# Where the weight parts, the normed rows and the activations lie in SBUF, in a four-layer decoder trunk

## The chip, the cores and the metric

The kernel runs on one core of one Trainium2 chip, as one launch. The metric is the device time of that launch in microseconds (us). The kernel before was timed three times: 1962.36, 1965.19 and 1966.22 us, median 1965.19 us. Shorter is better. All durations below come from one further execution that the hardware profiler recorded; its span is 1960.8 us.

## What is computed

Four decoder layers on 256 tokens of 1024 features, all in float32. Each layer is half a SwiGLU feed-forward, a token mixer, and another half feed-forward; a norm closes the trunk. The mixers are stick-breaking attention (layers 0 and 3), MoBA attention (layer 1) and latent attention (layer 2). Cut to what matters here:

```python
D_MODEL, SEQ, DEPTH, D_FF = 1024, 256, 4, 2816
def swiglu(x, w_gate_up, w_down):
    g, u = jnp.split(x @ w_gate_up, 2, axis=-1)
    return (jax.nn.silu(g) * u) @ w_down

for i in range(DEPTH):
    h = h + 0.5 * swiglu(rms_norm(h, norm_ffn1[i]), ffn1_w_gate_up[i], ffn1_w_down[i])
    h = h + mixer_i(rms_norm(h, norm_mix[i]))          # kind i mod 3
    h = h + 0.5 * swiglu(rms_norm(h, norm_ffn2[i]), ffn2_w_gate_up[i], ffn2_w_down[i])
return rms_norm(h, final_norm)
```

The weights are about 340 MB of float32, read once. The eight feed-forwards hold most of them and most of the products.

## The kernel before, in words

**Split products.** TensorE takes operands of the type float32r. Each float32 value is split into a high part (its rounding to float32r) and a low part (the rest), and a product of two float32 values becomes three products of parts: high by high, high by low, low by high. The hidden state `h` lies transposed, features on the 128 partitions and the 256 tokens along the columns.

**Weights.** A `Chunk` is up to 1 MB of one weight matrix. Its DMA lands in one of four buffers `raw` (8192 bytes in each partition). ScalarE then writes the high parts to a buffer `whi` (L314), VectorE subtracts and writes the low parts to a buffer `wlo` (L321). A `whi` and a `wlo` (4096 bytes in each partition) are taken and given back as a pair; there are six such pairs, in the list `parts`.

**Feed-forward.** `ffn` computes 22 column blocks of gate and up from the normed rows `x2`, then 8 row blocks of the output from the activations `a2`. Both tiles hold, for each row block of 128 features, 256 columns of high parts and then 256 columns of low parts. The helper `wide` issues two products for a 128x128 piece of weights: the piece's high part stays in the array while all 512 columns of the row block stream through (L434), then its low part while the 256 high columns stream (L435). This text calls the two a *pair*. The kernel has 4224 pairs. Each product is preceded by a load of its 128x128 weights (LDWEIGHTS, the rows of PEld), 512 bytes in each partition.

**Mixers.** `mm3` does the three products one by one, 256 columns each (L428, L429, L430; 512 such triples), for queries, keys and the output projection. `x_proj` does it the other way round: 128 columns of the normed rows are loaded as weights, and up to 512 columns of `whi` or `wlo` stream (L475, L476, L477; 232 triples).

**Order.** `Program` is a list scheduler: it puts all instructions of all engines in order by estimated costs before anything is built. The addresses of tiles play no part in it. DMAs are issued by SyncE.

**Addresses.** Tiles are laid out one after the other in the order in which `cp.tile` is called, each rounded up to 32 bytes. Nearly all tiles have sizes that are multiples of 512 bytes. The tile `gh` (gains and `h`) has 8628 bytes, and `x2` and `a2` follow it. In the built program a partition's addresses are therefore:

| tile | before: address, and modulo 1024 | after: address, and modulo 1024 |
|---|---|---|
| whi0 | 49280, 128 | 49280, 128 |
| wlo0 | 53376, 128 | 73920, 192 |
| whi1, wlo1 | 57472, 128 and 61568, 128 | 53376, 128 and 78016, 192 |
| x2 | 151104, 576 | 98496, 192 |
| a2 | 167488, 576 | 114880, 192 |

All six `whi` agree modulo 1024 with the first, all six `wlo` too, and row blocks of `x2` and `a2` are 2048 bytes apart. A 128x128 piece of weights starts at a multiple of 512 bytes within its buffer.

The program is allocated here:

## Time and profile before

| what | value |
|---|---|
| median of three timed runs | 1965.19 us (1962.36 to 1966.22) |
| span of the profiled execution | 1960.8 us |
| TensorE products busy | 1946.6 us, 99% |
| TensorE weight loads busy | 1696.5 us, 87% |
| VectorE busy | 1452.3 us, 74% |
| ScalarE busy | 1144.1 us, 58% |
| mean rate of the DMAs | 175 GB/s, q1 50.6% of 16 engines |
| granted TensorE clock | 0.998 of full speed |

How to read it: PE are products, PEld their weight loads, DVE is VectorE, ACT ScalarE. A product is drawn from when its columns enter until its last result is out, so successive products overlap in the table of times, and the duration of one is longer than the distance from its start to the next start. That distance, the *step*, is what a product costs when TensorE never idles. The chain of waits follows the work that ended last back to its beginning.

### The profile page before, as it was taken

The page shows a single profiled execution, that of the slowest core. Times are in us where ns is not written, and L with a number is a line of the kernel's source. Part 1 is how long each engine was busy: PE and PEld are TensorE (multiplying, and loading weights), DVE is VectorE, ACT ScalarE, POOL GpSimd, SP SyncE. Part 2 cuts the span into 40 slices and gives each one's busy share as a digit, 9 for nine tenths or more (in the row PEclk, how much of TensorE's full clock was granted, in tenths as well). Part 3 has the DMA queues.
Part 4 walks back from the last instruction along what each step waited for, and adds up shares of the span by engine and source line. Part 5 has one row for each costly group of instructions (what it writes and reads, how often), then busy time and mean ns, then how long its engine had stood idle before and what let it go on. Part 6 is the DMA issues. An engine that isn't in the chain of part 4 may idle for free.

```text
span 1960.8 us, 30578 instructions
## 1 busy us (share of the span) xinstructions
PE 1946.6 (99%) x11681; PEld 1696.5 (87%) x11681; DVE 1452.3 (74%) x2661; ACT 1144.1 (58%) x2119; POOL 0.4 (0%) x5
## 2 busy tenths in 40 slices
PE   9999999999999999999999999999999999999997
PEld 7888989888888878888888888988888888898886
DVE  8777767777777777877677768877677766668864
ACT  7555556555555555655555557755555555665553
POOL 0000000000000000000000000000000000000000
PEclk9999999999999999999999999999999999999999
DMA  8546435546654653554655454355465456435542
GB/s 301 184 146 220 163 129 175 191 147 204 208 181 147 221 181 109 178 188 147 214 199 191 141 178 155 126 197 178 151 213 197 165 168 220 148 125 198 177 151 81
DMA packets 55875, 342.79 MB, mean 175 GB/s; under 512 B 6192, under 2 KB 7088, under 8 KB 26928
## 3 DMA queue, kind: packets, MB, share of 16 engines
q1 hardware_dynamic: 55728, 340.84, 50.6%
q8 instruction: 92, 1.51, 0.3%
q14 instruction: 55, 0.45, 0.1%
HBM read 339.76 MB, written 1.05 MB: 174 GB/s over the span
## 4 chain that ended last, share of the span: by engine, by line
PE 98%; ACT 1%; DVE 0%; DMA 0%; SPq 0%; issue 0%; DVEq 0%; ACTq 0%
PE ps L434 50%; PE ps L435 26%; PE ps L428 3%; PE ps L429 3%; PE ps L430 3%; PE ps L475 3%; PE ps L476 2%; PE ps L477 2%; PE ps L574 1%; PE ps L624 1%; PE ps L733 1%; PE ps L698 1%; PE ps L771 1%; PE ps L596 1%; PE ps L562 0%; PE ps L576 0%
## 5 line engine op out<-in xcount | busy, mean ns | idle before, releaser
L314 ACT ACTIVATE whi<-raw 128x1024 fp32r<-128x1024 f32 (+2 forms) x738 | 703.0, 954 | 729.7 <-PE ps L434 527.3
L321 DVE TENSOR_TENSOR wlo<-raw,whi 128x1024 fp32r<-128x1024 f32 (+2 forms) x738 | 804.2, 1091 | 396.7 <-ACT whi L314 388.6
L434 PE MATMUL ps<-x,whi 128*128 128x512 f32 x2816 | 998.3, 398 | 1.0 <-DVE acc L345 0.8
L435 PE MATMUL ps<-x,wlo 128*128 128x256 f32 x2816 | 791.8, 281 | 0.2 <-DVE wlo L321 0.2
L434 PEld LDWEIGHTS ps<-x,whi 128*128 128x128 f32 x2816 | 529.7, 188 | 132.2 <-ACT whi L314 2.5
L435 PEld LDWEIGHTS ps<-x,wlo 128*128 128x128 f32 x2816 | 528.8, 188 | 1.3 <-DVE wlo L321 1.2
L434 PE MATMUL ps<-a,whi 128*128 128x512 f32 x1408 | 498.8, 398 | 0.0
L435 PE MATMUL ps<-a,wlo 128*128 128x256 f32 x1408 | 395.7, 281 | 0.0
L434 PEld LDWEIGHTS ps<-a,whi 128*128 128x128 f32 x1408 | 264.8, 188 | 65.1
L435 PEld LDWEIGHTS ps<-a,wlo 128*128 128x128 f32 x1408 | 264.4, 188 | 0.0
L443 DVE TENSOR_TENSOR mid<-ps,mid 128x256 f32<-128x256 f32 x416 | 173.5, 417 | 9.6 <-ACT mid L442 9.6
L442 ACT ACTIVATE mid<-ps 128x256 f32<-128x256 f32 x416 | 151.3, 367 | 11.9 <-PE ps L435 11.9
L515 DVE TENSOR_TENSOR mid<-mid 128x256 f32<-128x256 f32 x176 | 74.6, 424 | 14.2 <-DVE mid L443 0.5
L510 DVE TENSOR_TENSOR mid<-mid,rb 128x256 f32<-128x256 f32 x176 | 74.7, 424 | 6.4 <-ACT rb L411 0.9
L475 PE MATMUL ps<-whi,x 128*128 128x512 f32 (+2 forms) x192 | 74.4, 388 | 0.0
L517 DVE TENSOR_TENSOR a<-mid,a 128x256 fp32r<-128x256 f32 x176 | 73.4, 418 | 1.0 <-ACT a L516 1.0
L428 PE MATMUL ps<-a,whi 128*128 128x256 f32 x256 | 73.9, 289 | 0.0
L428 PE MATMUL ps<-x,whi 128*128 128x256 f32 x256 | 73.0, 285 | 0.0
L476 PE MATMUL ps<-wlo,x 128*128 128x512 f32 (+2 forms) x192 | 72.9, 380 | 0.0
L511 ACT ACTIVATE mid<-mid 128x256 f32<-128x256 f32 x176 | 71.8, 408 | 1.8 <-DVE mid L510 1.7
L477 PE MATMUL ps<-whi,x 128*128 128x512 f32 (+2 forms) x192 | 72.7, 379 | 0.0
L429 PE MATMUL ps<-a,whi 128*128 128x256 f32 x256 | 71.5, 279 | 0.0
(128 smaller groups left out, 1636.7 us busy)
## 6 DMA issues: line engine op xcount, KB each, us to landing
raw<-in_ffn_gu SPq DMA_DIRECT2D x173, 1024.0 KB, 4.8
raw<-in_ffn_dn SPq DMA_DIRECT2D x128, 704.0 KB, 4.1
raw<-in_sb_qk SPq DMA_DIRECT2D x16, 1024.0 KB, 4.9
raw<-in_moba_qkv SPq DMA_DIRECT2D x12, 1024.0 KB, 4.8
raw<-in_sb_v SPq DMA_DIRECT2D x8, 1024.0 KB, 4.7
raw<-in_sb_o SPq DMA_DIRECT2D x8, 1024.0 KB, 4.7
raw<-in_moba_o SPq DMA_DIRECT2D x4, 1024.0 KB, 4.8
raw<-in_mla_o SPq DMA_DIRECT2D x4, 1024.0 KB, 5.0
```

The costliest lines, as they stand in the source:

```text
L314: return lambda: nc.scalar.activation(b.ap[0][:, (k - i) * w:(e - i) * w], raw.ap[:, k * w:e * w], AF.Copy)
L321: nc.vector.tensor_sub(b.ap[1][:, s], raw.ap[:, k * w:e * w], b.ap[0][:, s].bitcast(F32))
L428: nc.tensor.matmul(o, wh, mh, start=first, stop=False, skip_group_check=True)
L429: nc.tensor.matmul(o, wh, ml, start=False, stop=False, skip_group_check=True)
L434: nc.tensor.matmul(o, wh, m2.rearrange("p a b -> p (a b)"), start=first, stop=False, skip_group_check=True)
L435: nc.tensor.matmul(o[:, :SEQ], wl, m2[:, 0, :], start=False, stop=last, skip_group_check=True)
L442: x = g.act(SEQ, lambda: nc.scalar.activation(o(), b.ap[:, SEQ:], AF.Copy), [last], take=take, lead=lead)
L443: return g.dve(SEQ, lambda: nc.vector.tensor_add(o(), b.ap[:, :SEQ], o()), [x], free=[b], lead=lead)
L475: nc.tensor.matmul(o, xs[0][:, k, ts], hi, start=(k == 0), stop=False)
L476: nc.tensor.matmul(o, xs[0][:, k, ts], lo, start=False, stop=False)
L477: nc.tensor.matmul(o, xs[1][:, k, ts], hi, start=False, stop=(k == n - 1))
L510: o = g.dve(SEQ, lambda: nc.vector.tensor_mul(x(), x(), rb[:, 0, :]), [o, rbs[0]])
```

## The change

It moves three groups of tiles. The six `whi` are allocated together; then comes an unused tile `shift` of 16 float32 (64 bytes in each partition); then the six `wlo`; then `x2` and `a2`, which stood behind `gh`. All tiles behind them move along; the total grows by 64 bytes. The number, shape and pairing of the buffers stay. No instruction is added or taken out, and the instructions of each engine stand in the same order as before, tile for tile. The rest of the diff drops comments and docstrings.

```diff
     raws = room(4, [MAXC], "raw")
-    parts = Slots([(cp.tile([P, HALF], F32R, name=f"whi{i}"), cp.tile([P, HALF], F32R, name=f"wlo{i}"))
-                   for i in range(6)])
+    whi = [cp.tile([P, HALF], F32R, name=f"whi{i}") for i in range(6)]
+    cp.tile([P, 16], F32, name="shift")
+    wlo = [cp.tile([P, HALF], F32R, name=f"wlo{i}") for i in range(6)]
+    parts = Slots(zip(whi, wlo))
+
+    x2 = cp.tile([P, NT, 2, SEQ], F32R, name="x2")
+    a2 = cp.tile([P, NF, 2, SEQ], F32R, name="a2")
     mids = room(3, [2 * ZC], "mid")
...
     h = gh[:, G_ALL:].rearrange("p (a b) -> p a b", a=NT)
-    x2 = cp.tile([P, NT, 2, SEQ], F32R, name="x2")
-    a2 = cp.tile([P, NF, 2, SEQ], F32R, name="a2")
     xh, xl = x2[:, :, 0, :], x2[:, :, 1, :]
```

## Rows read from the trace of the kernel before

**Rows 1.** The page: busy shares of the engines, and the chain of waits.

```profile
PE 1946.6 (99%) x11681; PEld 1696.5 (87%) x11681; DVE 1452.3 (74%) x2661; ACT 1144.1 (58%) x2119; POOL 0.4 (0%) x5
...
PE 98%; ACT 1%; DVE 0%; DMA 0%; SPq 0%; issue 0%; DVEq 0%; ACTq 0%
PE ps L434 50%; PE ps L435 26%; PE ps L428 3%; PE ps L429 3%; PE ps L430 3%; PE ps L475 3%; PE ps L476 2%; PE ps L477 2%; PE ps L574 1%; PE ps L624 1%; PE ps L733 1%; PE ps L698 1%; PE ps L771 1%; PE ps L596 1%; PE ps L562 0%; PE ps L576 0%
```

**Rows 2.** Groups by line: group, count | busy us, mean ns | idle before, releaser.

```profile
L321 DVE TENSOR_TENSOR wlo<-raw,whi 128x1024 fp32r<-128x1024 f32 x456 | 557.5, 1224 | 229.9 <-ACT whi L314 228.0
L434 PE MATMUL ps<-x,whi 128*128 128x512 f32 x2816 | 998.3, 398 | 1.0 <-DVE acc L345 0.8
L434 PE MATMUL ps<-a,whi 128*128 128x512 f32 x1408 | 498.8, 398 | 0.0
```

**Rows 3.** Waits: who waited for whom, us in total, times, longest.

```profile
ACT whi L314 <- PE ps L434: 527.3, 482, 3.2
...
PEld ps L434 <- ACT whi L314: 2.5, 3, 1.1
```

**Rows 4.** Timeline, products in a feed-forward: start us, duration us, what.

```profile
59.79 0.40 PE L434 MATMUL ps<-x,whi 128*128 128x512 f32 x1
60.02 0.28 PE L435 MATMUL ps<-x,wlo 128*128 128x256 f32 x1
60.14 0.40 PE L434 MATMUL ps<-x,whi 128*128 128x512 f32 x1
...
62.97 0.40 PE L434 MATMUL ps<-x,whi 128*128 128x512 f32 x1
```

**Rows 5.** Timeline, products and weight loads at 400 us, another feed-forward.

```profile
400.12 0.40 PE L434 MATMUL ps<-x,whi 128*128 128x512 f32 x1
...
400.12 0.19 PEld L435 LDWEIGHTS ps<-x,wlo 128*128 128x128 f32 x1
400.36 0.19 PEld L434 LDWEIGHTS ps<-x,whi 128*128 128x128 f32 x1
```

**Rows 6.** Timeline, output projection of layer 0 (mm3), from 299.82 us.

```profile
299.82 0.28 PE L428 MATMUL ps<-a,whi 128*128 128x256 f32 x1
...
301.94 0.28 PE L428 MATMUL ps<-a,whi 128*128 128x256 f32 x1
```

**Rows 7.** Timeline, queries and keys of layer 0 (mm3), from 272.61 us.

```profile
272.61 0.28 PE L428 MATMUL ps<-x,whi 128*128 128x256 f32 x1
272.72 0.28 PE L429 MATMUL ps<-x,whi 128*128 128x256 f32 x1
...
274.65 0.28 PE L428 MATMUL ps<-x,whi 128*128 128x256 f32 x1
```

**Rows 8.** Timeline, values of layer 0 (x_proj), from 250.75 us.

```profile
250.75 0.39 PE L475 MATMUL ps<-whi,x 128*128 128x512 f32 x1
250.99 0.39 PE L476 MATMUL ps<-wlo,x 128*128 128x512 f32 x1
251.22 0.39 PE L477 MATMUL ps<-whi,x 128*128 128x512 f32 x1
251.44 0.39 PE L475 MATMUL ps<-whi,x 128*128 128x512 f32 x1
...
252.82 0.39 PE L475 MATMUL ps<-whi,x 128*128 128x512 f32 x1
```

**Rows 9.** Timeline, weight loads of four products of one column each.

```profile
18.73 0.53 PEld L403 LDWEIGHTS ps<-onesf,acc 128*128 128x128 f32 x4
```

**Rows 10.** Stretches: from:to, length, busy time by engine, clock, DMA share.

```profile
59.79:62.97 3.18, 3.18 (x21) 2.76 (x19) 2.32 (x4) 1.99 (x5) 0.00 (x0) 1.00 0.20 31
272.52:274.56 2.04, 2.04 (x21) 2.04 (x20) 1.97 (x6) 0.77 (x2) 0.00 (x0) 1.00 0.00 0
299.82:301.94 2.12, 2.12 (x20) 2.12 (x19) 1.92 (x5) 2.04 (x4) 0.00 (x0) 1.00 1.02 429
310.00:680.00 370.00, 370.00 (x2102) 321.59 (x2102) 275.30 (x469) 212.45 (x379) 0.00 (x0) 1.00 0.55 187
```

## The prediction

> **What bounds the kernel now.** I read the page's busy shares and its chain of waits first [rows 1]: products are busy 99% of the span, and the chain is TensorE for 98%, of which the two lines of `wide` hold 76 points (50% and 26%). VectorE comes next with 74%. Then the waits [rows 3]: the longest is ScalarE's, 527.3 us, for TensorE to give weight buffers back. TensorE's loads waited for a high part in 2.5 us altogether. So weights stand ready, and TensorE sets the end by its own pace.

> That pace is read from the starts of successive products. Nine pairs of `wide` go from 59.79 to 62.97 us [rows 4], 353.3 ns a pair, some 235 ns for the 512 columns and 118 ns for the 256. [...]

> It is not a fixed price of these shapes. A triple of `mm3` streams the same 768 columns, and takes 353.3 ns in one place (six triples from 299.82 to 301.94 us [rows 6]) and 340.0 ns in another (six from 272.61 to 274.65 us [rows 7]). Lines, tiles and shapes are alike, and the clock is 1.00 in both [rows 10]. In `x_proj` nine products of 512 columns take 2.07 us [rows 8], 230 ns each, and one of them goes from 251.22 to 251.44 us, against 235 in `wide`. [...] The other engines' load does not sort the places: the fast one has VectorE at 97% and no DMA, the slow one has VectorE at 91%, ScalarE at 96% and full DMA, and the feed-forward loses as much as the slow one with DMA at 20% [rows 10]. What always runs along is TensorE's own weight load: the next one starts with the product, to 0.01 us [rows 5].

> **The change part by part.** No instruction is added, removed or moved, so no term comes from queues or order. What changes is distance. By the table of addresses, the moving row starts 448 bytes beyond the weights that are loaded meanwhile, modulo 512, that is 64 bytes short of them, for high and low parts alike. Afterwards it is 64 bytes beyond a high part and exactly level with a low part. In `wide`, the 512-column product runs beside the load of a low part and the 256-column product beside the load of a high part [rows 5]. So the long product goes from 64 short to level, the short one from 64 short to 64 beyond.

> *The pairs.* No trace here shows `wide` at these distances, so I bound its new step. The nearest row for 64 beyond is `x_proj`: there the weights stream and the normed rows are loaded, so the stream is 64 bytes beyond the load today. Its 512-column products take 230 ns on average instead of 235 [rows 8]. The nearest row for the 256-column product is the fast place of `mm3`, 113.3 ns each [rows 7]. That is also the least it can be: four loads in a row occupy 0.53 us, the last alone 0.19, so a load goes out every (0.53 - 0.19) / 3 = 0.113 us [rows 9], and every 256-column product hides one. [...] Adding up what rows do show, 226 to 230 for the long one and 113.3 for the short one, gives 339 to 343 ns. I take 340.0, since 340.0 and 353.3 are the two values at which the same 768 columns are seen to settle, 51 and 53 times 6.67 ns. One step of 6.67 ns more or less is 4224 x 6.67 = 28.2 us, and I count the sizes of all cases in such steps. Saved: 4224 x 13.33 = 56.3 us.

> *The mixers.* In `mm3` the distances become 64 beyond, level, 64 beyond; in `x_proj` they turn from 64 beyond to 64 short, level, 64 short. If the distances matter as above, `mm3` gains and `x_proj` loses. Bounds: all 512 triples of `mm3` by 13.3 ns either way is 6.8 us; all 232 triples of `x_proj` from 230 to 235 ns a product, 15 ns a triple, is 3.5 us of loss. I take zero for the sum, between ends of 7 us of gain and 10 us of loss.

> *Other engines.* The largest split takes VectorE 1224 ns for 1024 columns [rows 2]; `raw` and `whi` keep their starts modulo 1024, only the target moves. I cost it at nothing: it is hidden behind TensorE. In the long feed-forward stretch from 310 to 680 us VectorE is busy 275 of 370 us [rows 10]; at 340 / 353.3 of the time its share rises from 74% to 77%. The DMAs would go from a share of 0.55 to 0.57. Neither becomes the bound.

> [...]

> *The sum.* 1960.8 - 56.3 = 1904.5 us of span. The median of the timed runs lies 4.4 us above that span; I keep that: 1908.9, rounded to 1909 us.

> **The rivals.** *No effect.* The two places of `mm3` have the same tiles, and so the same distances, and yet differ by 13.3 ns [rows 6, 7]. So address alone does not set the pace; the moment at which a run of products begins does. If that is all, pairs fall into the 353.3 ns that two feed-forwards at 59 and 400 us both show, and the time is 1965 us, give or take 3. For it: two places, one layout, two paces; a layout that stays a multiple of 64 bytes throughout. Against it: `wide` is always at the slow value, and `x_proj`, with the other distance, is below its 235 ns. [...]

> *Slower.* Level is the worst distance: the low part's load and the long product begin together [rows 5] and then start in the same place modulo 512, on every pair. [...] With one more, a pair takes 360.0 ns and the kernel 1965.2 + 28.2 = 1993 us; with two, the difference between the two paces of `mm3` in the other direction, 366.7 ns and 2022 us. It decides as soon as the long product's step passes some 242 ns with the short one unchanged. For it: level exists nowhere in the kernel before for these operands, so nothing excludes it. Against it: a product whose columns pass faster than the weights are loaded (512 columns in 235 ns against 128 in 113 [rows 4, 9]) runs ahead at once and need not meet the load again.

> *More.* Both products come near their least: 220 ns and 113.3 ns, 333.3 ns a pair, 20 ns less, 84.5 us. The time would be 1881 us. For it: one step of about 220 ns in `x_proj` [rows 8]. Against it: no stretch of any kind keeps it up.

> *Less.* One step of 6.67 ns is won, 346.7 ns a pair: 1937 us. It belongs to the forecast's side.

> **How the numbers follow.** Forecast, two steps won, 1909 us (1898 to 1920 with the mixers' ends): 0.27. One step won or only part of the pairs changed, 1925 to 1955: 0.14. Three steps or more, 1881 and below: 0.10. No effect: 0.28. Slower by one step or part of it: 0.12; by two or more: 0.09. The gaining side together holds 0.51, and the likeliest single size on it is the forecast; it and no effect are nearly level, and I choose the forecast because three kinds of rows (the fast triples, the shorter steps of `x_proj`, the loads' 0.113 us) show paces below what `wide` runs at, and none shows a reason in the work itself why `wide` should not reach them. The range must reach both neighbours: from 1881 us (three steps won) to 1994 us (one step lost). Left out are two steps lost and more than three won, under 2 in 10; on the gaining side alone the range would be 1881 to 1957. A measurement of this kernel tells about 0.2% (3.9 us) from no change, as its three runs lie within 3.9 us. Faster 0.51, same 0.28, slower 0.21.

> **What would show it.** In the trace after, ten pairs should take 3.40 us from start to start, in all eight feed-forwards; the split into the long and the short step tells which distance did it. 353.3 everywhere would show that the load's distance is nothing to the pace, 360 or 366.7 that level is bad. The share of VectorE should rise to about 77% with no wait of TensorE on `whi` or `wlo`; if TensorE's loads wait for L321 in more than a few us, the weights no longer keep up. `x_proj` above 230 ns a product beside faster pairs would confirm that 64 short costs more than 64 beyond. The prediction is wrong at its root if pairs come to both paces in different feed-forwards: then the beginning decides, and the layout does not.

## The result and the profile after

The changed kernel takes 1938.43 us, the median of four runs (1938.17 to 1939.94); the kernel before, beside it, 1965.09 us. The ratio is 0.987, with a 95% interval of 0.986 to 0.989. That is 26.7 us less, where 56 had been forecast: the direction was right, the size a little under half.

The profiled execution of the changed kernel has a span of 1938.2 us, 22.6 less than the 1960.8 of before. (Each profile is one execution. That of before lies below the median of its kernel, that of after above; the four us between 22.6 and 26.7 are no more than single executions of one kernel differ by, 1962.36 to 1966.22 us.) In the code after the change `wide` is L438 and L439, `mm3` L432 to L434, `x_proj` L479 to L481, the splits L318 and L325.

The page of the changed kernel, busy shares, the chain by engine, and the group of the long products (busy us, mean ns, idle before and its releaser):

```profile
PE 1923.2 (99%) x11681; PEld 1690.6 (87%) x11681; DVE 1450.9 (75%) x2661; ACT 1145.8 (59%) x2119; POOL 0.4 (0%) x5
...
PE 98%; ACT 1%; DVE 0%; DMA 0%; SPq 0%; issue 0%; DVEq 0%; ACTq 0%
...
L438 PE MATMUL ps<-x,whi 128*128 128x512 f32 x2816 | 979.5, 394 | 1.8 <-DVE acc L349 1.6
```

Beside [rows 1, 2], everything has kept its place. TensorE is still 98% of the chain and all counts are the same. The wait of ScalarE for weight buffers is still the longest, and a little shorter than the 527.3 us of [rows 3], which fits a TensorE that gives buffers back sooner:

```profile
ACT whi L318 <- PE ps L438: 498.0, 448, 3.0
```

So what changed is the pace of the products. The stretches of the changed kernel (from:to, length, then busy time of PE, PEld, VectorE, ScalarE, GpSimd, granted clock, DMA share, GB/s), two pieces of two feed-forwards each:

```profile
310.00:680.00 370.00, 370.00 (x2129) 324.30 (x2128) 278.63 (x474) 214.56 (x381) 0.00 (x0) 1.00 0.55 189
1290.00:1640.00 350.00, 350.00 (x2094) 311.82 (x2093) 268.30 (x456) 208.87 (x368) 0.00 (x0) 1.00 0.56 191
```

Before, 370 us held 2102 products from 310 us on [rows 10], 5.68 per us. Now they hold 2129, 5.75 per us, and the later stretch 2094 / 350 = 5.98 per us. The clock is 1.00 in both, the DMA share and VectorE's share (75% and 77%) are alike. The two places of one kernel have two paces, which the timeline shows (start us, duration us, what), the first and last of ten pairs each:

```profile
400.30 0.40 PE L438 MATMUL ps<-x,whi 128*128 128x512 f32 x1
...
403.80 0.40 PE L438 MATMUL ps<-x,whi 128*128 128x512 f32 x1
...
1400.11 0.39 PE L438 MATMUL ps<-a,whi 128*128 128x512 f32 x1
...
1403.51 0.39 PE L438 MATMUL ps<-a,whi 128*128 128x512 f32 x1
```

Ten pairs take 3.50 us at 400 us, 350.0 ns a pair, and 3.40 us at 1400 us, 340.0 ns a pair. Before, it was 353.3 ns in every feed-forward ([rows 4] show one place). Taken over all pairs that another pair follows (4196, from start to start), 2579 run at 350.0 ns, 1552 at 340.0 ns, and the mean is 347.9 ns against 354.5 before. That is 6.54 ns x 4224 = 27.6 us of gain.

The mixers gave some of it back. The output projection of layer 0 after the change, nine triples of `mm3`:

```profile
297.83 0.28 PE L432 MATMUL ps<-a,whi 128*128 128x256 f32 x1
...
301.01 0.28 PE L432 MATMUL ps<-a,whi 128*128 128x256 f32 x1
```

3.18 us, 353.3 ns a triple, is the slow pace of [rows 6]. The fast pace of [rows 7], 340.0 ns, which 175 triples had before, is gone: 427 of 468 triples go at 347 to 360 ns, the mean rises from 356.5 to 362.0 ns, and 512 x 5.5 ns = 2.8 us are lost. In `x_proj` of the changed kernel one triple now goes from 251.69 to 252.40 us:

```profile
251.69 0.40 PE L481 MATMUL ps<-whi,x 128*128 128x512 f32 x1
...
252.40 0.39 PE L481 MATMUL ps<-whi,x 128*128 128x512 f32 x1
```

That is 0.71 us for three products of 512 columns, against 0.69 in [rows 8] (three products from 250.75 to 251.44 us). The mean of these triples rises from 700.4 to 712.9 ns, which over some 200 of them is 2.5 us. The balance is 27.6 - 2.8 - 2.5 = 22.3 us, against 22.6 us between the two spans.

### The profile page after: what moved, and what is told of

Its sections match the earlier page's. It is cut to its first block, busy times and chain, and to the rows that moved or that the text cites. A ratio compares the mean times of both kernels' runs of the same rounds, so it can differ in the third digit from the quotient of the medians.

```text
span 1938.2 us, 30578 instructions
## 1 busy us (share of the span) xinstructions
PE 1923.2 (99%) x11681; PEld 1690.6 (87%) x11681; DVE 1450.9 (75%) x2661; ACT 1145.8 (59%) x2119; POOL 0.4 (0%) x5
## 4 chain that ended last, share of the span: by engine, by line
PE 98%; ACT 1%; DVE 0%; DMA 0%; SPq 0%; issue 0%; DVEq 0%; ACTq 0%
PE ps L438 50%; PE ps L439 25%; PE ps L432 3%; PE ps L434 3%; PE ps L433 3%; PE ps L479 3%; PE ps L480 3%; PE ps L481 2%; PE ps L578 1%; PE ps L628 1%; PE ps L737 1%; PE ps L702 1%; PE ps L775 1%; PE ps L600 1%; PE ps L566 0%; PE ps L580 0%
## 5 line engine op out<-in xcount | busy, mean ns | idle before, releaser
L318 ACT ACTIVATE whi<-raw 128x1024 fp32r<-128x1024 f32 (+2 forms) x738 | 703.3, 954 | 702.1 <-PE ps L438 498.0
L325 DVE TENSOR_TENSOR wlo<-raw,whi 128x1024 fp32r<-128x1024 f32 (+2 forms) x738 | 803.8, 1090 | 372.4 <-ACT whi L318 360.3
L438 PE MATMUL ps<-x,whi 128*128 128x512 f32 x2816 | 979.5, 394 | 1.8 <-DVE acc L349 1.6
L439 PE MATMUL ps<-x,wlo 128*128 128x256 f32 x2816 | 786.2, 279 | 0.2 <-DVE wlo L325 0.2
L438 PEld LDWEIGHTS ps<-x,whi 128*128 128x128 f32 x2816 | 529.9, 188 | 120.1 <-ACT whi L318 3.5
L439 PEld LDWEIGHTS ps<-x,wlo 128*128 128x128 f32 x2816 | 529.4, 188 | 1.2 <-DVE wlo L325 1.1
L438 PE MATMUL ps<-a,whi 128*128 128x512 f32 x1408 | 489.0, 393 | 0.0
L439 PE MATMUL ps<-a,wlo 128*128 128x256 f32 x1408 | 392.7, 279 | 0.0
L438 PEld LDWEIGHTS ps<-a,whi 128*128 128x128 f32 x1408 | 264.6, 188 | 58.6
L439 PEld LDWEIGHTS ps<-a,wlo 128*128 128x128 f32 x1408 | 264.3, 188 | 0.0
L479 PE MATMUL ps<-whi,x 128*128 128x512 f32 (+2 forms) x192 | 75.2, 392 | 0.0
L432 PE MATMUL ps<-a,whi 128*128 128x256 f32 x256 | 73.7, 288 | 0.0
L432 PE MATMUL ps<-x,whi 128*128 128x256 f32 x256 | 73.0, 285 | 0.0
L481 PE MATMUL ps<-whi,x 128*128 128x512 f32 (+2 forms) x192 | 72.9, 380 | 0.0
L434 PE MATMUL ps<-a,wlo 128*128 128x256 f32 x256 | 72.4, 283 | 0.0
```

What stands on the lines that cost most here:

```text
L318: return lambda: nc.scalar.activation(b.ap[0][:, (k - i) * w:(e - i) * w], raw.ap[:, k * w:e * w], AF.Copy)
L325: nc.vector.tensor_sub(b.ap[1][:, s], raw.ap[:, k * w:e * w], b.ap[0][:, s].bitcast(F32))
L432: nc.tensor.matmul(o, wh, mh, start=first, stop=False, skip_group_check=True)
L434: nc.tensor.matmul(o, wl, mh, start=False, stop=last, skip_group_check=True)
L438: nc.tensor.matmul(o, wh, m2.rearrange("p a b -> p (a b)"), start=first, stop=False, skip_group_check=True)
L439: nc.tensor.matmul(o[:, :SEQ], wl, m2[:, 0, :], start=False, stop=last, skip_group_check=True)
```

## The experiments

Three things are to be explained: that addresses matter at all, which of the distances does it, and why one layout has two paces. A kernel's layout is given below by two numbers, in bytes: how far a moving row starts beyond a piece of a high part, and beyond a piece of a low part, modulo 512. Before it is (-64, -64), after (+64, 0). In `wide` the first stands for the short product of 256 columns and the second for the long one of 512 [rows 5].

At the start there were these theories. A: only the long product counts, and level with the low part's load is good. B: only the short product counts, and 64 beyond the high part's load is good. C: it is the grouping of the buffers, not the distance. D, which came up with e3: each of the two products wants a distance of its own. Later ones are told where they arise. The paces that all runs gave stand here together. "Pair" is the mean over all pairs, with the paces at which most of them settle. The triples of `mm3` are given by their mean, those of `x_proj` (512 columns) by the value at which most of them settle. All are worked out from the starts of the products in each trace.

| kernel | layout | pair: mean; settles at (ns) | `mm3` (ns) | `x_proj` (ns) | total (us) |
|---|---|---|---|---|---|
| before | -64, -64 | 354.5; 353.3 | 356.5 | 687 | 1965.09 |
| after | +64, 0 | 347.9; 350.0 and 340.0 | 362.0 | 698 to 709 | 1938.43 |
| e1_no_pad | 0, 0 | 349.1; 346.7, first run 353.3 | 367.4 | 680 | 1945.54 |
| e2_pad_behind | +64, +64 | 353.0; 348.9, later 353.3 | 360.9 | 697 to 703 | 1960.69 |
| e3_swap | 0, +64 | 348.1; 346.7 | 361.7 | 687 | 1939.05 |
| e4_order_only | -64, -64 | 354.6; 353.3 | 355.7 | 687 | 1962.74 |
| e5_short_of_high | -64, 0 | 347.6; 340.0, 350.0, 353.3 | 362.3 | 697 to 703 | 1938.60 |
| e6_256_high | 256, 0 | 349.1; 346.7, first run 353.3 | 367.4 | 680 | 1945.71 |
| e7_256_both | 256, 256 | 348.3; 346.7 | 367.4 | 680 | 1941.69 |
| e12_128_high | 128, 0 | 353.3; 352.0 | 363.2 | 687 | 1960.75 |

Kernels told without an interval were run once, beside a run of the kernel before on the same chip, which took 1963.1 to 1965.6 us.

### Is it the distance, and which

**The grouping alone.** High parts, low parts, then `gh`, `x2`, `a2`: the new grouping at the old distances.

```diff
     whi = [cp.tile([P, HALF], F32R, name=f"whi{i}") for i in range(6)]
-    cp.tile([P, 16], F32, name="shift")
     wlo = [cp.tile([P, HALF], F32R, name=f"wlo{i}") for i in range(6)]
+    gh = cp.tile([P, G_ALL + NT * SEQ], F32, name="gh")
...
-    gh = cp.tile([P, G_ALL + NT * SEQ], F32, name="gh")
```

> High parts together, low parts together, then gh, then the moving rows: the order of the changed kernel, but the distances of the kernel before (64 short of both parts, moving rows at 576 modulo 1024). Theories A and B: pairs at 353.3 ns throughout, 1965 us. Theory C: pairs at 350 and 340 ns, 1938 us.

Its timeline (as in all fences of this section: start us, duration us, what), the first and the last of ten pairs:

```profile
399.98 0.40 PE L437 MATMUL ps<-x,whi 128*128 128x512 f32 x1
...
403.51 0.40 PE L437 MATMUL ps<-x,whi 128*128 128x512 f32 x1
```

3.53 us, the 353.3 ns of before, in all feed-forwards, and 1962.74 us beside 1965.62. Theory C falls: tiles in a new order, at the old distances, run as before. Between this kernel and the changed one only addresses differ, so addresses are what is worth 24 us.

**Without the 64 bytes.** All operands level.

```diff
-    cp.tile([P, 16], F32, name="shift")
```

> The pad is taken out, so high parts, low parts and moving rows are all level modulo 512. Theory A (the long product's distance to the low part counts, and level is good): pairs of wide at 350 ns or less in all feed-forwards, as in the changed kernel or better. Theory B (the short product's distance to the high part counts, and 64 beyond is good): pairs back at 353.3 ns or above, some 1965 us or more. Theory C (which tiles stand together, not the 64 bytes): pairs as in the changed kernel, 350 and 340 ns, 1938 us.

Ten pairs and, in the output projection of layer 0, three triples of `mm3`, from the timeline of this kernel:

```profile
299.67 0.28 PE L431 MATMUL ps<-a,whi 128*128 128x256 f32 x1
...
300.75 0.28 PE L431 MATMUL ps<-a,whi 128*128 128x256 f32 x1
...
400.23 0.39 PE L437 MATMUL ps<-x,whi 128*128 128x512 f32 x1
...
403.69 0.39 PE L437 MATMUL ps<-x,whi 128*128 128x512 f32 x1
```

3.46 us, 346.7 ns a pair: most of the gain without the pad, at 1945.54 us. (The first long run of pairs, 487 of them, goes at 353.3 ns all the same; the other seven at 346.7.) Level is not bad for the long product. It is for the short one: a triple of `mm3` takes 360.0 ns, 120.0 for each of its three products of 256 columns, and its mean of 367.4 is the highest in the table. For 512 columns it is the other way round: in `x_proj` the triple takes 680 ns, 226.7 a product, its best. 226.7 + 120.0 make the 346.7 of the pair, though the pair itself splits into 230 and 117. So the two products want opposite things, which speaks for D. It speaks against B, by which nothing should have been gained with the short product at level; A could still stand, though it had expected 350 ns or less in all feed-forwards.

**The pad behind the low parts.** Both distances 64 beyond.

```diff
     whi = [cp.tile([P, HALF], F32R, name=f"whi{i}") for i in range(6)]
-    cp.tile([P, 16], F32, name="shift")
     wlo = [cp.tile([P, HALF], F32R, name=f"wlo{i}") for i in range(6)]
+    cp.tile([P, 16], F32, name="shift")
```

> The pad stands behind the low parts, so the moving rows are 64 bytes beyond both parts. Theory A: the low part is no longer level, pairs return to 353.3 ns, some 1965 us. Theory B: pairs at 350 ns or less, 1938 us or less. Theory C: as in the changed kernel, 1938 us.

Two places of its timeline, ten pairs each:

```profile
400.00 0.40 PE L438 MATMUL ps<-x,whi 128*128 128x512 f32 x1
...
403.49 0.39 PE L438 MATMUL ps<-x,whi 128*128 128x512 f32 x1
...
1050.20 0.39 PE L438 MATMUL ps<-x,whi 128*128 128x512 f32 x1
...
1053.73 0.40 PE L438 MATMUL ps<-x,whi 128*128 128x512 f32 x1
```

349 ns at 400 us and 353 ns at 1050 us: the mean is 348.9 ns in the first three feed-forwards, 353.3 in the later ones, 1960.69 us in all. With the short product as in the changed kernel, the gain is nearly gone as soon as the long one leaves the level, as A and D have it and B has not. And here, too, one layout has more than one pace.

**The parts exchanged.** The low parts first, then the pad, then the high parts: the short product level, the long one 64 beyond.

```diff
-    whi = [cp.tile([P, HALF], F32R, name=f"whi{i}") for i in range(6)]
-    cp.tile([P, 16], F32, name="shift")
     wlo = [cp.tile([P, HALF], F32R, name=f"wlo{i}") for i in range(6)]
+    cp.tile([P, 16], F32, name="shift")
+    whi = [cp.tile([P, HALF], F32R, name=f"whi{i}") for i in range(6)]
```

> Low parts first, pad, high parts, moving rows: level with the high part, 64 beyond the low part, the changed kernel's two distances exchanged. Theory A: 353.3 ns or more. Theory B: 353.3 ns or more. Theory C: 1938 us. If pairs are faster than 350 ns here, none of the three holds and each product wants its own distance.

The timeline of this kernel, ten pairs:

```profile
400.01 0.40 PE L438 MATMUL ps<-x,whi 128*128 128x512 f32 x1
...
403.47 0.40 PE L438 MATMUL ps<-x,whi 128*128 128x512 f32 x1
```

Ten pairs take 3.46 us, 346.7 ns each, and the total is 1939.05 us. I had not expected that: the long product is off the level and the pair still runs at 346.7 ns, as 233.3 + 113.3. So A falls, and B too, since the short product is level here. D survives in a weaker form only: what the pair takes follows from both distances together, and prices of single products cannot simply be added.

**Short of the high parts.** `gh` in the place of the pad: the short product stays at -64 as before, only the long one goes to level. Theory E said that -64 is what spoils the short product.

```diff
-    cp.tile([P, 16], F32, name="shift")
+    gh = cp.tile([P, G_ALL + NT * SEQ], F32, name="gh")
...
-    gh = cp.tile([P, G_ALL + NT * SEQ], F32, name="gh")
```

> High parts, gh, low parts, moving rows: 64 bytes short of the high part, level with the low part. Theory D (each product wants its own distance: the long one level with the low part, the short one away from level with the high part, on either side): a pair takes 230 ns for the long product as with everything level, and 113 to 118 ns for the short one as in mm3 of the kernel before, 343 to 348 ns in all, 1920 to 1942 us. Theory E (64 beyond is what the short product wants, 64 short is the bad side): 350 ns or more, 1950 us or more.

Two places of its timeline, ten pairs each:

```profile
1050.23 0.40 PE L437 MATMUL ps<-x,whi 128*128 128x512 f32 x1
...
1053.76 0.40 PE L437 MATMUL ps<-x,whi 128*128 128x512 f32 x1
...
1400.24 0.39 PE L437 MATMUL ps<-a,whi 128*128 128x512 f32 x1
...
1403.64 0.39 PE L437 MATMUL ps<-a,whi 128*128 128x512 f32 x1
```

They take 3.53 us at 1050 us, and 3.40 us at 1400 us. With 2045 pairs at 340.0 ns, E falls. D had the total right, but not the paces: four long runs go at 340.0 ns, two at 350.0 and two at 353.3, and only their mean, 347.6, lies where D had every pair. The total, 1938.60 us, is that of the changed kernel, without its pad. This is also the closest comparison of all. Against e4 the `whi`, `x2` and `a2` keep their addresses; only the `wlo` and `gh` have changed places, and that is worth 24 us. So here moving the long product to level is what pays. It is no rule, as e3 gains as much without it, and e12 below shows level without the gain.

**256 and 128 bytes.** `krope`, a tile of 256 bytes, as the pad, between the parts or behind them, and a pad of 128 bytes.

```diff
-    cp.tile([P, 16], F32, name="shift")
+    krope = cp.tile([P, 2, MLA_ROPE], F32, name="krope")
...
-    krope = cp.tile([P, 2, MLA_ROPE], F32, name="krope")
```

> High parts, krope (256 bytes), low parts, moving rows: 256 bytes from the high part, the farthest modulo 512, and level with the low part. Theory D, if what counts is being away: 346.7 ns or less for a pair, 1938 us or less. If only 64 beyond helps the short product: 347 to 353 ns, with the short product at 117 ns or more as with everything level.

For e7 the same `krope` stands behind the low parts instead.

> The moving rows 256 bytes from both parts. Theory D with being away as the good for the short product alone: long product at 233 ns or more, short one at 113 to 118 ns, 346 to 353 ns a pair, 1938 to 1965 us. If being far away is good for both: 340.0 ns or less, 1910 us or less.

```diff
-    cp.tile([P, 16], F32, name="shift")
+    cp.tile([P, 32], F32, name="shift")
```

> A pad of 128 bytes in place of 64: 128 bytes from the high part, level with the low part. If distances count modulo 256 (256 bytes gave what level gave), 128 is the farthest from level: pairs between 340 and 347 ns, 1910 to 1940 us, if being away from level is what the short product wants. If they count modulo 128: 346.7 ns, as with everything level, 1945 us.

The timeline of the kernel with 256 bytes between the parts, ten pairs:

```profile
400.13 0.39 PE L437 MATMUL ps<-x,whi 128*128 128x512 f32 x1
...
403.60 0.39 PE L437 MATMUL ps<-x,whi 128*128 128x512 f32 x1
```

It is the kernel without a pad once more, in the pair's 346.7 ns, in the triple's 367.4 and in the total (1945.71 against 1945.54 us); with 256 bytes behind the parts it is 346.7 ns and 1941.69 us, the first long run included, which at 353.3 ns costs the other two kernels 487 x 6.67 ns = 3.2 us. So a distance of 256 bytes acts as none, and the prediction's count modulo 512 was too wide. Whether all distances repeat after 256 bytes was not tried. The timeline of the kernel with 128 bytes:

```profile
400.27 0.39 PE L438 MATMUL ps<-x,whi 128*128 128x512 f32 x1
...
403.79 0.39 PE L438 MATMUL ps<-x,whi 128*128 128x512 f32 x1
```

3.52 us, 352.0 ns, 1960.75 us: the long product is level, the short one away from level, and nearly all of the gain is lost. Neither of the two expected outcomes came. "Away from level" is therefore not what the short product wants, and 128 is neither level nor 64. I have no rule that gives all these values. Nor was everything moved together: in every kernel the first group of parts starts at 128 modulo 1024, so that it is the distance alone, whatever the addresses themselves, is not shown.

### Two paces in one layout

In the changed kernel each long run of pairs begins behind the norm, whose last work on TensorE is two transpositions (L412). The eight such runs hold 361 to 515 pairs each. Those that begin at 24.22, 323.91, 507.93, 811.09 and 995.10 us go on at 350.0 ns, those at 1278.28, 1457.22 and 1756.10 us at 340.0 ns, each to its end. Two of these beginnings, in the timeline of the changed kernel:

```profile
323.66 0.28 PE L439 MATMUL ps<-x,wlo 128*128 128x256 f32 x1
323.78 0.38 PE L412 MATMUL ps<-identf,ny 128*128 128x128 f32 x2
323.91 0.48 PE L438 MATMUL ps<-x,whi 128*128 128x512 f32 x1
...
324.69 0.40 PE L438 MATMUL ps<-x,whi 128*128 128x512 f32 x1
...
325.39 0.40 PE L438 MATMUL ps<-x,whi 128*128 128x512 f32 x1
...
1278.03 0.28 PE L439 MATMUL ps<-x,wlo 128*128 128x256 f32 x1
1278.15 0.38 PE L412 MATMUL ps<-identf,ny 128*128 128x128 f32 x2
1278.28 0.47 PE L438 MATMUL ps<-x,whi 128*128 128x512 f32 x1
...
1279.06 0.39 PE L438 MATMUL ps<-x,whi 128*128 128x512 f32 x1
...
1279.75 0.39 PE L438 MATMUL ps<-x,whi 128*128 128x512 f32 x1
```

The rows read alike; only the next two pairs take 0.70 us here and 0.69 there. In the trace's nanoseconds, from the last product before the interruption to the first one behind it, the five stretches at 350.0 begin after 250 or 256 ns, the three at 340.0 after 255 ns. So theory F: the moment at which a run restarts picks one of the paces that the layout offers. Its rival G: the place in the program does, 340.0 being found in the later feed-forwards alone. (In e5, with as many products in the interruption, long runs at 340.0 begin as early as 24.02 us, which speaks against G. There 254 ns lead to 340.0 four times and to 353.3 twice, and 250 ns to 350.0 twice.)

**One transposition more.** The norm repeats its second transposition, so that every run restarts later by one product of 128 columns. Nothing that is computed changes. (Ten norms have these transpositions, those of the eight feed-forwards and of two mixers, so the trace has ten products more, 1.1 us of work.)

```diff
-            for t in range(2):
+            for t in (0, 1, 1):
```

> The changed kernel's layout, and one product of 128 columns (about 0.11 us) more in the norm ahead of each feed-forward, which repeats a transposition: 0.9 us of work in all. Theory F (the moment at which a feed-forward's run of pairs begins chooses between the two paces of one layout): the feed-forwards that run at 350 ns and those at 340 ns change, so the total leaves 1938 us by up to 17 us down or 10 us up. Theory G (the pace hangs on the place in the program, its data or its buffers): 350 ns up to the latent mixer and 340 ns behind it, 1939 us.

Ten pairs, and the beginning of the run behind layer 0's mixer, in its timeline:

```profile
318.89 0.28 PE L439 MATMUL ps<-x,wlo 128*128 128x256 f32 x1
319.01 0.49 PE L412 MATMUL ps<-identf,ny 128*128 128x128 f32 x3
319.25 0.47 PE L438 MATMUL ps<-x,whi 128*128 128x512 f32 x1
...
400.26 0.39 PE L438 MATMUL ps<-x,whi 128*128 128x512 f32 x1
...
403.66 0.39 PE L438 MATMUL ps<-x,whi 128*128 128x512 f32 x1
```

The interruption has three products, and 365 ns instead of 250 to 256. Behind it ten pairs take 3.40 us at 400 us, where the changed kernel took 3.50. 4074 of 4196 pairs now run at 340.0 ns, in every feed-forward, and the total is 1915.70 us. More work makes the kernel 23 us faster, more than the 17 us that F had allowed, since all five runs at 350.0 change and the three at 340.0 stay. G falls: the early places are as fast as the late ones.

The same kernel was timed:

> The kernel of e8_one_more again, timed. Theory F (the moment chooses the pace, and chooses it alike in each execution): 1914 to 1918 us in all runs, ratio to the kernel before 0.974 to 0.977. If the choice differs from execution to execution: scattered between 1910 and 1945 us.

1914.29 us, the median of four runs (1913.8 to 1916.13), beside 1963.71 us for the kernel before: a ratio of 0.975, with an interval of 0.973 to 0.976. The four runs lie within 2.4 us, so the choice falls nearly alike in each execution. It beats both kernels, and at a mean of 341.5 ns a pair it has nearly the pace that the prediction had given to the change by itself.

**The same transposition in the kernel before.**

> The kernel before with the same product more in each norm, its layout unchanged (64 bytes short of both parts). If the faster pace needs the new distances: pairs stay at 353.3 ns and the time at 1965 us plus about 1 us. If the moment alone could have given it: pairs at 340 ns in some feed-forwards, less than 1950 us.

Ten pairs in the timeline of that kernel:

```profile
399.98 0.40 PE L434 MATMUL ps<-x,whi 128*128 128x512 f32 x1
...
403.51 0.40 PE L434 MATMUL ps<-x,whi 128*128 128x512 f32 x1
```

3.53 us, 353.3 ns a pair as ever, and its time is 1964.69 us against 1963.71. The additional product does nothing at the old distances. So in these kernels layout and restart do different things: the layout decides which paces are to be had, the restart which of them a run falls into. At the old distances (before, e4, e10) all 24 long runs go at 353.3 ns, behind interruptions of 252 to 254 and of 362 or 363 ns; others were not tried there.

**Two more, and other lengths.** If the moment alone decided, a further shift should bring some runs back to 350.0. Theory H, by contrast: an additional product in itself, a longer pause, brings 340.0. Two transpositions more shift the restart by about 0.22 us, and a plain product of 96, 98, 100 or 102 columns behind the two transpositions was meant to shift it in small steps (`n` in the second diff).

```diff
-            for t in range(2):
+            for t in (0, 1, 1, 1):
```

> The changed kernel's layout with two products of 128 columns more in each of those norms (about 0.22 us). Theory F: the feed-forwards' paces are chosen anew, each 350 or 340 ns, total between 1913 and 1948 us, and another pattern by feed-forward than with none or one. If one more product is itself what brings 340 ns (a pause that clears something): 340.0 ns throughout again, 1917 us.

```diff
             for t in range(2):
                 nc.tensor.transpose(c.ap[:, t * P:(t + 1) * P], r["r"][:, t:t + 1].to_broadcast([P, P]), identf)
+            nc.tensor.matmul(c.ap[:, SEQ:SEQ + n], identf, identf[:, :n], start=True, stop=True, skip_group_check=True)
```

> The changed kernel's layout; in each feed-forward's norm one float32 product of 96 columns more, into an unused half of the bank, behind the two transpositions. Four kernels differ only in its columns (96, 98, 100, 102), that is in the moment at which the long run of pairs begins again, by some 3 ns from one to the next. Theory F (the moment chooses the pace): at least one of the four has feed-forwards at 350 ns and at least one has the others at 340 ns, totals between 1914 and 1950 us. Theory H (an additional product in itself brings 340 ns): all four 340.0 ns throughout, 1914 to 1918 us.

> The same with 98 columns. Theory F: a pattern of its own of 350 and 340 ns by feed-forward. Theory H: 340.0 ns throughout, 1914 to 1918 us.

> The same with 100 columns. Theory F: a pattern of its own of 350 and 340 ns by feed-forward. Theory H: 340.0 ns throughout, 1914 to 1918 us.

> The same with 102 columns. Theory F: a pattern of its own of 350 and 340 ns by feed-forward. Theory H: 340.0 ns throughout, 1914 to 1918 us.

| kernel | interruption (ns) | long runs at 340.0 | total (us) |
|---|---|---|---|
| after | 250, 255 or 256 | 3 of 8 | 1938.43 |
| e8_one_more | 365 | 8 of 8 | 1915.70 |
| e11_two_more | 474 | 8 of 8 | 1916.88 |
| e13, 96 / 98 / 100 / 102 columns | 478 to 480 | 8 of 8 in each | 1917.09 / 1915.36 / 1915.01 / 1917.79 |

The four widths did not do what they were made for: the restart moved by 2 ns between them, where some 3 ns from one to the next had been the author's estimate. (Each of these plain float32 products stands in the trace as two, as each of the two of the norm's sums does, L407 below with x4, so their interruption holds four products, as e11's does, and lasts 478 to 480 ns beside its 474.) So they are no test of fine steps, and what holds the restart there was not shown. In all 48 long runs of these six kernels the added products lead to 340.0 ns, as H expected and F did not.

But neither the length of the interruption nor the number of its products is what brings 340.0. The norm ahead of each long run interrupts the pairs a few us earlier, too, for its sums: four products of one column (L407). In the same trace of e11:

```profile
314.28 0.50 PE L407 MATMUL ps<-onesf,acc 128*128 128x1 f32 x4
...
315.08 0.40 PE L438 MATMUL ps<-x,whi 128*128 128x512 f32 x1
...
318.58 0.40 PE L438 MATMUL ps<-x,whi 128*128 128x512 f32 x1
...
318.93 0.60 PE L412 MATMUL ps<-identf,ny 128*128 128x128 f32 x4
...
320.07 0.39 PE L438 MATMUL ps<-x,whi 128*128 128x512 f32 x1
...
323.47 0.39 PE L438 MATMUL ps<-x,whi 128*128 128x512 f32 x1
```

Behind the sums ten pairs take 3.50 us, 350.0 ns each; behind the transpositions 3.40 us, 340.0 each. Both interruptions hold four products, and in the trace's nanoseconds they last 475 or 476 ns (sums) and 473 to 475 (transpositions) throughout this kernel. In all six kernels the 48 short runs behind the sums, of 7 or 11 pairs, go at 350.0. In the changed kernel five of eight do, behind 475 or 476 ns, and three, behind 481 or 482 ns, go at 340.0. So H falls as a matter of pause or of count, and a few ns turn the pace within one kernel and one kind of interruption, as F has it. F gives no rule for which moment leads where, though, and the pace ahead of the interruption may have a part: in the changed kernel the sums lead to 350.0 where 340.0 went before, and to 340.0 where 350.0 did. With kind and pace ahead alike, only five of its long runs differ: they go at 350.0 behind 256 ns twice, and at 340.0 behind 255 ns three times. What sets the pace within that ns stays open.

## Why the prediction was half right

**What held.** *The bound:* TensorE sets the end by its own pace, and with unchanged counts and a clock of 1.00 the time fell by what its steps fell (22.3 us of steps, 22.6 us of span). *The cause, in part:* the pace hangs on where the moving rows and the weight parts lie (e4 against e5 and against the changed kernel, 24 us by addresses alone). *The products:* the long one gained most (its mean step is 231.3 ns, over both paces, against 235.9 before; the short one's 116.6 against 118.6). *The other engines at nothing:* VectorE went from 74% to 75%, to 77% where pairs run at 340.0, as worked out, and TensorE's loads of the long products waited 3.5 us for high parts, against 2.5. *`x_proj`:* 64 short costs more than 64 beyond, as the last part of the prediction said: 687 ns a triple before, 698 to 709 after, where two of its three products are 64 short and one is level.

**The step that failed** is the term of the pairs: "I take 340.0, since 340.0 and 353.3 are the two values at which the same 768 columns are seen to settle". The term was -13.33 ns x 4224 = -56.3 us, and it measured -6.54 ns x 4224 = -27.6 us. It has two faults. The choice was made between the two values that `mm3` shows at the old distances, with other whole steps of 6.67 ns left to the rivals; the runs have 346.7, 348.9, 350.0 and 352.0 besides, and 350.0 is no whole number of 6.67 ns (two pairs are, at 105 of them). And one layout was given one pace. Yet [rows 6, 7] had shown two paces in one layout, which the prediction spent on the rival of no effect instead of on its own term. In the trace 1552 of 4196 pairs come to 340.0 and 2579 stay at 350.0. What came is the prediction's case "one step won or only part of the pairs changed", 1925 to 1955 us, to which it gave 0.14. That its rival *Less* names 1937 us, 1.4 from the measured time, is luck: its pace of 346.7 ns is found nowhere in the changed kernel's long runs. A small slip changed nothing: the "one step of about 220 ns" in `x_proj` is 225 ns in the trace's own nanoseconds, shortened by rounding to 0.01 us.

**The mixers at zero** were off by 5.3 us, inside the ends of 7 us of gain and 10 of loss. `x_proj` lost as expected; `mm3` was expected to gain if anything, and lost its 340.0 pace instead.

**The rivals.** *No effect* had part of the mechanism beside the wrong conclusion: the way in which a run of products begins does set its pace, but among those of its layout. The prediction called itself "wrong at its root if pairs come to both paces in different feed-forwards: then the beginning decides, and the layout does not". They did come to two paces, 350.0 and 340.0, and still the layout decides as well, as the additional transposition shows, worth 24 us at the new distances and nothing at the old ones. *Slower*, with level the worst distance, is refuted for the long product (in the kernel without a pad 226.7 ns for 512 columns in `x_proj`, and 230 in the pair against 235 before) and has something for the short one (there 120.0 ns for 256 columns in `mm3`, its highest mean of all layouts). The one or two steps of 6.67 ns that it put on each pair are shown by no run: with both products level a pair takes 346.7 ns in seven of the eight long runs (e1), with the long one alone level 340.0 to 353.3 ns (the changed kernel, e5, e12).

**What was not isolated.** The same instructions in the same order, loads included, take 353.3, 352.0, 350.0, 346.7 or 340.0 ns a pair by the addresses of the tiles (and, within a layout, by the restart). That it is the loads which the moving rows meet was the author's supposition, and it was not isolated, since no kernel here ran pairs without loads. What is shown is that the addresses count: 24 us between e4 and e5, in which only `wlo` and `gh` have changed places.

## What to carry to other kernels

When TensorE hardly idles (99% busy here) and one shape runs at more than one step (here the same 768 columns in 340.0 and in 353.3 ns), compare its steps across the whole trace, and the starts of the moving rows with those of the weight tiles: a pad of 64 bytes with another order of allocation, or such an order alone (e5), was worth 1.3% here, and 2.5% with one small product added. Try several layouts, since no rule found here tells the good ones. Expect more than one steady pace per layout (350.0 and 340.0 ns in the changed kernel), taken up where a run of products restarts behind an interruption, and before forecasting a pace, count how many runs are likely to come to it. A change of layout moves every product that uses the tiles, so the shapes that lose (here `mm3` and `x_proj`, 5 us) belong in the sum.
